# Both mixers' output products as seven half-size products, in a two-layer fp32 decoder kernel on one NeuronCore

## The chip, the core and the metric

One core of one Trainium2 chip runs the whole kernel. The metric is device time in microseconds (us) of one execution. A profiled execution is a further run, and its trace gives the start and end of every instruction on the engines PE (matrix products), PEld (its weight loads), DVE (vector), ACT (scalar, activations), POOL (GpSimd) and SP (which issues most transfers).

## What is computed

A decoder trunk of two layers on 512 positions of width 1024, in fp32. Each layer has three sub-layers, each wrapped as `x = x + RMSNorm_post(f(RMSNorm_pre(x)))`: a mixer, attention into 256 memory rows, and a SwiGLU feed-forward. The change touches the mixers' last product, `[..] @ w_out`, and the stage behind it, the keys and values of the memory.

```
def fox_shortconv_mixer(h, w_in, b_f, conv_w, w_out):      # layer 0
    ...
    y_b = b_gate * causal_depthwise_conv(c_gate * u, conv_w)
    return jnp.concatenate([y_a, y_b], axis=-1) @ w_out
def rglru_mixer(h, w_in, conv_w, conv_b, w_a, b_a, w_i, b_i, lam, w_out):   # layer 1
    gate, u = jnp.split(h @ w_in, 2, axis=-1)
    ...
    y = jax.nn.gelu(gate) * hs.astype(h.dtype)
    return y @ w_out
def memory_cross_attention(h, m, w_q, w_kv, w_o):
    q = (h @ w_q).reshape(bsz, seq, MEM_HEADS, MEM_HEAD_DIM)
    k, v = jnp.split(m @ w_kv, 2, axis=-1)
    ...
```

## The kernel before

**Products.** Every fp32 operand is split into a rounded high half and the rest, `lo = v - hi` (`split_out`, L539: ACT rounds, DVE subtracts), and a product is three matmuls, hi·hi, hi·lo and lo·hi. Weights come through four `st` buffers (SP's queue) and are split into pools `wh` and `wl` of four buffers each; a load of 128 x 1024 values is one `st`. PSUM is used as two sets of four banks, `bankA` and `bankB`.

**Order.** PE's instructions run in the order of the code. DVE, ACT and POOL are put in order by a scheduler at build time, except in a few stretches that are written out by hand (layer 1's mixer is one). SP issues loads in order, each as soon as its `st` buffer is free.

**Layer 0's mixer** (`fox`). Products of the input weights, the short convolution (`conv`) and the attention's 128-query blocks are woven: `main` yields products, `side` attention steps. The output product (`OutProj`, from L552) makes columns 0 to 511 first (`half0_steps`, 96 matmuls of 128x512: 8 k-blocks, 4 row tiles, 3 matmuls), as each quarter of `y` comes ready, then columns 512 to 1023 (`half1`, 96 more), with the post-norm of each row tile (`chain`), the next sub-layer's pre-norm (`next`) and its transposes (`transpose`) after each tile. The four loads of the second half are kept (`rh`, `rl`).

**Memory.** In layer 0 `memory_T` transposes the normalised memory rows on PE (`turn`, eight transposes each, L1001), writes them to DRAM for layer 1, and multiplies by `g_mem`. The two turns are called from `half1` behind its first two row tiles, and use `bankA`. `memory_kv` makes four chunks of 256 key columns (48 matmuls of 128x256 each), then the two remaining row tiles' transposes (`rest`), then the values (two halves of 48 matmuls of 128x512).

**Layer 1's mixer** (`rglru`). Column chunks of `c_w_in` are multiplied one after the other (`ws_gemm`), with the gates' products and the scan between; `gelu(n, ...)` makes 256 columns of `y`. After the last, `ws_gemm(w, 768, ..)`, the output product runs as in layer 0 with the bank sets exchanged.

**The feed-forward's down product** (`DownProj`, a subclass) is made in the form that the change brings to the mixers: seven products instead of eight, with weight sums `t1` to `t4` in DRAM. `plan` queues the sums' making: copies go to SP's queue between loads (`pace`: three for every four loads), adding transfers to POOL's queue (`spend`).

Of the kernel before, what the change touches and what calls it, by code (L numbers as in the profile page):

```python
# [42 lines left out]
def trunk_kernel(ctx: ExitStack, tc: tile.TileContext, a: dict, out: bass.AP):  # L43
# [103 lines left out]
    def spend(n, behind=None):  # L147
# [15 lines left out]
        ("gm", a["g_mem"].rearrange("l (m p) -> (l m) p", p=P)),  # L163
        ("gp", a["g_mix_pre"][1].rearrange("(m p) -> m p", p=P)),
    )
    off = {}
# [151 lines left out]

    def put_T_pair(hT, hss, j, gain):

        ps = bankB()
        for kk in range(2):
            for t in range(2):
                c = 2 * kk + t
                src = hss[t][j // 2][:, (j % 2 * 2 + kk) * P:(j % 2 * 2 + kk + 1) * P]
                nc.tensor.transpose(out=ps[:, c * P:(c + 1) * P], in_=src, identity=ident)
        ks = [(2 * j + kk, ps[:, kk * 256:kk * 256 + 256]) for kk in range(2)]
        for k, v in ks:
            nc.scalar.mul(out=hT.hi[k][:, 0:256], in_=v, mul=ch(gain, k))
        for k, v in ks:  # L330
            nc.vector.scalar_tensor_tensor(out=hT.lo[k][:, 0:256], in0=v, scalar=ch(gain, k), in1=f(hT.hi[k][:, 0:256]),
                                           op0=ALU.mult, op1=ALU.subtract)

# [324 lines left out]
    class DownProj(OutProj):  # L658
# [300 lines left out]
        def hook(self, m):  # L959
# [3 lines left out]
            elif m == 3:  # L963
                self.transpose(3)


    memT = dram.tile([P, KT, MEM], F32, name="memT")
# [54 lines left out]

    def memory_kv(layer, vhi, vlo, between):

# [14 lines left out]
        between()  # L1039
        vh, vl = group("vh"), group("vl")  # L1040
        for nh in range(2):
# [10 lines left out]
            for j in range(2):  # L1052
                split_out(banks[j], vh[:, 2 * j + nh, :], vl[:, 2 * j + nh, :])
        return kh, kl, vh, vl

# [148 lines left out]
    def fox(proj):  # L1204
# [124 lines left out]

        y = Feat([None] * KT, [None] * KT)  # L1330
        yg, qk, cs = {}, {}, {}
        done = set()
        TO = [(0, 0), (1, 0), (2, 0), (1, 384)]

        def y_group(m):
            if m not in yg:
                yg[m] = group("y")
                y.hi[m], y.lo[m] = yg[m][:, 0, :], yg[m][:, 1, :]
                y.hi[4 + m], y.lo[4 + m] = yg[m][:, 2, :], yg[m][:, 3, :]
            return yg[m]  # L1340

        def qk_pairs(m0):


            def put_q(banks):
                for i in range(2):
                    qk[m0 + i] = group("qk")
                    split_out(banks[i], qk[m0 + i][:, 0, :], qk[m0 + i][:, 1, :], -0.125)

            def put_k(banks):  # L1350
                for i in range(2):
                    split_out(banks[i], qk[m0 + i][:, 2, :], qk[m0 + i][:, 3, :])
                    done.add(("qk", m0 + i))

            yield from ws_steps(w, m0 * P, hT, put_q)
            yield from ws_steps(w, FOXW + m0 * P, hT, put_k)

        def attention(m):
# [53 lines left out]

            yt, tmp = sbuf("yt"), sbuf("tmp")
            for s in range(2):
# [11 lines left out]
                yield 1  # L1426
            gy = y_group(m)
            split_out(yt, gy[:, 0, :], gy[:, 1, :])
            done.add(("y", m))

        def conv(m0):
# [3 lines left out]
            def put_c(banks):  # L1435
                for i in range(2):
                    cs[m0 + i] = sbuf("cs")
                    nc.scalar.copy(out=cs[m0 + i], in_=banks[i])

            def put_u(banks):  # L1440
                for i in range(2):
                    c = cs[m0 + i]
                    t = sbuf("cu", 514)
                    nc.gpsimd.memset(t[:, 0:2], 0.0)
                    nc.vector.tensor_tensor(out=t[:, 2:514], in0=banks[i], in1=c, op=ALU.mult)
                    cw = [ch("scw", 4 * j + m0 + i) for j in range(3)]
                    nc.vector.tensor_scalar_mul(out=c, in0=t[:, 2:514], scalar1=cw[2])
# [7 lines left out]
            def put_b(banks):  # L1455
                for i in range(2):
                    c = cs[m0 + i]
                    nc.vector.tensor_tensor(out=c, in0=c, in1=banks[i], op=ALU.mult)
                    gy = y_group(m0 + i)
                    split_out(c, gy[:, 2, :], gy[:, 3, :])  # L1460

# [21 lines left out]
        for _ in qk_pairs(0):  # L1483
            pass
        proj.y = y
        weave(main(), side())


    def rglru(hT, prev, proj):
        w = a["c_w_in"][0]  # L1490
        U, PU, Q = {}, {}, {}
        y = Feat([None] * KT, [None] * KT)

# [16 lines left out]
        def gates(n):  # L1510
# [6 lines left out]
            for i in range(2):  # L1517
                for m in range(2):
# [5 lines left out]
                    banks[i, m] = ps  # L1524
            Qf, Pf = f(Q[n]), f(PU[n])
            for m in range(2):
                c = 2 * n + m
# [16 lines left out]
        def gelu(n, banks):  # L1544
            yg = group("y")
            Qf = f(Q[n])
            for m in range(2):
# [6 lines left out]
                nc.vector.scalar_tensor_tensor(out=s, in0=s, scalar=1.0, in1=gp, op0=ALU.add, op1=ALU.mult)  # L1554
                nc.vector.tensor_tensor(out=s, in0=s, in1=Qf[:, m, :], op=ALU.mult)
                split_out(s, yg[:, m, :], yg[:, 2 + m, :], 0.5)
                y.hi[2 * n + m], y.lo[2 * n + m] = yg[:, m, :], yg[:, 2 + m, :]

# [12 lines left out]
        gelu(2, ws_gemm(w, 512, hT))  # L1571
        gelu(3, ws_gemm(w, 768, hT))
        proj.y = y
        proj.half0(range(0, KT, 2), True, True)


    hT = prev = None
    for layer in range(2):
        hTc = new_hT() if layer else None
        pf = DownProj(layer, a["g_ffn_post"][layer], a["g_mix_pre"][1], None, layer == 1)  # L1580
        pf.follow_w = a["c_w_in"][0], (D, D + 256)
        pf.plan()
        pm = OutProj(a["ab_w_out"][0] if layer == 0 else a["c_w_out"][0], None, KT,
                     a["g_mix_post"][layer], a["g_cross_pre"][layer], hTc, *((bankA, bankB) if layer == 0 else (bankB, bankA)))
        if layer == 0:
            fox(pm)
            pm.hT = hTc = new_hT()
        else:
            rglru(hT, prev, pm)
        vhi, vlo, steps = memory_T(layer, pm.first)  # L1590
        pm.half1(steps)
        pm.next(NT - 1)
        spend(1)

        def rest():
            for t in (2, 3):
                pm.transpose(t)

        kv = memory_kv(layer, vhi, vlo, rest)
        hTf = new_quads()  # L1600
# [30 lines left out]
```

## Time and profile before

| | us |
|---|---|
| median of 3 runs | 1390.49 (1390.46 to 1390.69) |
| the profiled execution | 1390.6 |
| its span, first to last instruction | 1388.8 |
| mean granted PE clock, share of full | 0.996 |
| attention's last product to the memory's first transposes, layer 0 | 195.02 to 214.15 |
| layer 0's key products | about 234 to 257 |
| layer 1's output product, first to last matmul with `wh` | 842.0 to 863.1 |

Lines of the profile name an engine, a line, an operation and `out<-in`. Behind a group stand its count, busy time and mean nanoseconds, then the idle time of the engine ahead of it and what ended that. Matmuls overlap, so a matmul's own duration (0.39 us for 128x512) is longer than the distance between two starts, which is what one more costs.

### The profile page before, as it was taken

The page shows a single profiled execution, that of the slowest core. Times are in us where ns is not written, and L with a number is a line of the kernel's source. Part 1 is how long each engine was busy: PE and PEld are TensorE (multiplying, and loading weights), DVE is VectorE, ACT ScalarE, POOL GpSimd, SP SyncE. Part 2 cuts the span into 40 slices and gives each one's busy share as a digit, 9 for nine tenths or more (in the row PEclk, how much of TensorE's full clock was granted, in tenths as well). Part 3 has the DMA queues.
Part 4 walks back from the last instruction along what each step waited for, and adds up shares of the span by engine and source line. Part 5 has one row for each costly group of instructions (what it writes and reads, how often), then busy time and mean ns, then how long its engine had stood idle before and what let it go on. Part 6 is the DMA issues. An engine that isn't in the chain of part 4 may idle for free.

```text
span 1388.8 us, 21766 instructions
## 1 busy us (share of the span) xinstructions
PE 1375.6 (99%) x8416; PEld 1225.7 (88%) x8416; DVE 1110.5 (80%) x1801; ACT 725.3 (52%) x1187; POOL 111.7 (8%) x161
## 2 busy tenths in 40 slices
PE   8999999999999999999999999999999999999997
PEld 6778788988899999998889888988889999999886
DVE  6876677646589999989898999663568999999987
ACT  4354456434465444456674797453456444445663
POOL 1000002011010101000011000101200011000001
PEclk9999999999999999999999999999999999999999
DMA  6844452667424567566665657256812555666653
GB/s 225 277 156 158 139 178 66 210 158 148 106 92 137 155 158 186 159 231 229 196 220 178 223 169 248 82 185 153 166 61 92 168 152 174 153 176 239 208 188 132
DMA packets 155250, 233.62 MB, mean 168 GB/s; under 512 B 8477, under 2 KB 90497, under 8 KB 153866
## 3 DMA queue, kind: packets, MB, share of 16 engines
q1 hardware_dynamic: 134706, 180.25, 40.1%
q0 software_dynamic: 17072, 46.16, 15.2%
q10 hardware_dynamic: 3368, 5.82, 1.3%
q8 instruction: 66, 1.08, 0.3%
q14 instruction: 38, 0.31, 0.1%
HBM read 219.60 MB, written 58.74 MB: 200 GB/s over the span
## 4 chain that ended last, share of the span: by engine, by line
PE 98%; DMA 1%; issue 1%; DVE 0%; POOL 0%; SPq 0%; ACT 0%; DVEq 0%; POOLq 0%
PE bA L336 14%; PE bA L338 14%; PE bA L337 14%; PE bB L336 6%; PE bB L337 6%; PE bB L338 6%; PE bB L810 3%; PE bB L812 3%; PE bB L811 3%; PE bA L810 2%; PE bA L812 2%; PE bA L811 2%; PE bA L569 2%; PE bA L571 2%; PE bB L571 2%; PE bB L569 2%
## 5 line engine op out<-in xcount | busy, mean ns | idle before, releaser
L546 DVE TENSOR_TENSOR wl<-st,wh 128x1024 fp32r<-128x1024 f32 x108 | 131.2, 1221 | 96.2 <-ACT wh L545 94.9
L545 ACT CAST wh<-st 128x1024 fp32r<-128x1024 f32 x108 | 113.1, 1050 | 119.5 <-PE bA L337 70.2
L336 PE MATMUL bA<-hTh,wh 128*128 128x512 f32 (+1 forms) x448 | 171.4, 383 | 0.2 <-ACT hTh L314 0.2
L337 PE MATMUL bA<-hTl,wh 128*128 128x512 f32 (+1 forms) x448 | 167.8, 375 | 0.3 <-DVE hTl L315 0.3
L338 PE MATMUL bA<-hTh,wl 128*128 128x512 f32 (+1 forms) x448 | 168.1, 375 | 0.0
L437 ACT CAST wg<-wr 128x1024 fp32r<-128x1024 f32 x80 | 83.6, 1045 | 49.1 <-DVE wr L466 38.4
L776 ACT CAST wh<-st 128x1024 fp32r<-128x1024 f32 x76 | 74.9, 985 | 63.6 <-PE bA L812 27.0
L338 PEld LDWEIGHTS bA<-hTh,wl 128*128 128x128 f32 x448 | 84.3, 188 | 15.4
L438 DVE TENSOR_TENSOR wg<-wr,wg 128x1024 fp32r<-128x1024 f32 x80 | 97.1, 1214 | 0.0
L337 PEld LDWEIGHTS bA<-hTl,wh 128*128 128x128 f32 x448 | 84.6, 189 | 14.1 <-DVE hTl L315 0.5
L336 PEld LDWEIGHTS bA<-hTh,wh 128*128 128x128 f32 x448 | 84.5, 189 | 14.0 <-ACT hTh L314 0.5
L781 DVE TENSOR_TENSOR wl<-st,wh 128x1024 fp32r<-128x1024 f32 x76 | 86.1, 1133 | 10.2 <-ACT wh L776 10.2
L437 ACT CAST wh<-tt 128x1024 fp32r<-128x1024 f32 x40 | 42.1, 1053 | 61.4 <-DVE tt L466 61.4
L336 PE MATMUL bA<-hTq,wh 128*128 128x256 f32 x208 | 59.2, 284 | 0.0
L338 PE MATMUL bA<-hTq,wl 128*128 128x256 f32 x208 | 58.8, 283 | 0.0
L337 PE MATMUL bA<-hTq,wh 128*128 128x256 f32 x208 | 58.8, 283 | 0.0
L810 PE MATMUL bB<-wh,ya 128*128 128x512 f32 x148 | 57.6, 389 | 0.0
L811 PE MATMUL bB<-wl,ya 128*128 128x512 f32 x148 | 57.6, 389 | 0.0
L812 PE MATMUL bB<-wh,ya 128*128 128x512 f32 x148 | 57.6, 389 | 0.0
L756 DVE TENSOR_TENSOR ya<-yb,ya 128x512 fp32r<-128x512 f32 x84 | 53.3, 638 | 0.0
L810 PE MATMUL bA<-wh,ya 128*128 128x512 f32 x132 | 51.3, 389 | 0.0
L811 PE MATMUL bA<-wl,ya 128*128 128x512 f32 x132 | 51.3, 389 | 0.0
(375 smaller groups left out, 4428.4 us busy)
## 6 DMA issues: line engine op xcount, KB each, us to landing
wr<-in_w_ffn_gu_dram SPq DMA_DIRECT2D x80, 512.0 KB
st<-t SPq DMA_DIRECT2D x40, 512.0 KB
t<-in_w_ffn_down_dram SPq DMA_DIRECT2D x32, 512.0 KB
st<-in_w_xkv_dram SPq DMA_DIRECT2D x32, 512.0 KB
st<-in_w_ffn_down_dram SPq DMA_DIRECT2D x30, 512.0 KB
st<-in_ab_w_in_dram SPq DMA_DIRECT2D x24, 512.0 KB
y<-yr POOLq DMA_DIRECT2D x18, 512.0 KB, 3.9
t<-in_w_ffn_down_dram POOLq DMA_DIRECT2D x16, 512.0 KB, 8.7
```

The lines of the kernel that those rows point to most:

```text
L336: nc.tensor.matmul(out=ps, lhsT=wh, rhs=xh, start=first, stop=False)
L337: nc.tensor.matmul(out=ps, lhsT=wh, rhs=xl, start=False, stop=False)
L338: nc.tensor.matmul(out=ps, lhsT=wl, rhs=xh, start=False, stop=last)
L437: return (lambda: nc.scalar.copy(out=to[0], in_=src), lambda: nc.vector.tensor_tensor(out=to[1], in0=src, in1=f(to[0]), op=ALU.subtract))
L438: lambda: nc.vector.tensor_tensor(out=to[1], in0=src, in1=f(to[0]), op=ALU.subtract))
L545: nc.scalar.copy(out=hi, in_=src)
L546: nc.vector.tensor_tensor(out=lo, in0=src, in1=f(hi), op=ALU.subtract)
L776: nc.scalar.copy(out=self.wt[s][0], in_=self.st[s])
L781: nc.vector.tensor_tensor(out=lo, in0=self.st[s], in1=f(hi), op=ALU.subtract)
L810: nc.tensor.matmul(out=banks[t], lhsT=yh, rhs=wh[:, jj, :], start=first and jj == 0, stop=False)
L811: nc.tensor.matmul(out=banks[t], lhsT=yh, rhs=wl[:, jj, :], start=False, stop=False)
L812: nc.tensor.matmul(out=banks[t], lhsT=yl, rhs=wh[:, jj, :], start=False, stop=last and jj == n - 1)
```

## The change

Both output products become a `MixProj`. With the mixer's output cut into row halves 1, 2 and inner halves 1, 2 (`a11` to `a22`) and the weights likewise (`b11` to `b22`), seven products of 256 rows, 512 inner and 512 columns are formed (24 matmuls of 128x512 each, 168 in all where there were 192) from `n3 = a21 - a11`, `s2 = a22 - n3`, `n1 = a11 - s2`, `n4 = a12 - s2` and the weight sums. They are made in fourteen pieces of twelve matmuls:

| pieces | 0, 1 | 2, 3 | 4, 6 | 5, 7 | 8, 9 | 10, 11 | 12, 13 |
|---|---|---|---|---|---|---|---|
| product | a11·b11 | n3·t3 | a22·t4 | a12·b21 | s2·t2 | n1·t1 | n4·b22 |

Each piece loads and splits one 128 x 1024 block of weights: fourteen splits where there were eight. The sums take eight copies and eight adds per mixer. Activations: DVE makes the differences and splits each of the seven operands; after the products it combines them (`q`, `v`, `c21`, `p1`). The norm steps behind that (`tail`) are called between the key chunks of `memory_kv` (c = 0 to 3) and after the first half of the values; the gain of the next pre-norm is applied at the transposes, by channel, so that its own load is gone.

In layer 0 pieces take the place of `half0_steps`; a11, n3, a22, a12 lie in `bankA`, s2, n1, n4 in `bankB`, and the memory's turns go on using `bankA`. In layer 1 pieces 0 and 1 go ahead of `ws_gemm(w, 768, ..)`, and the sets are exchanged. The first key chunk's weights are loaded ahead (`ahead`).

```diff
+    class MixProj(DownProj):
+        PIECES = tuple((n, j) for n in ("a11", "n3") for j in range(2)) + tuple(
+            (n, j) for j in range(2) for n in ("a22", "a12")) + tuple((n, j) for n in ("s2", "n1", "n4") for j in range(2))
+        B = {"a11": "b11", "n3": "t3", "a22": "t4", "a12": "b21", "s2": "t2", "n1": "t1", "n4": "b22"}
...
+        SUMS = {"n3": ("a21", "a11"), "s2": ("a22", "n3"), "n1": ("a11", "s2"), "n4": ("a12", "s2")}
...
+        def plan(self):
+            for to, frm, add in (("t3", "b12", "b22"), ("t2", "b11", "t3"), ("t4", "b21", "t2"), ("t1", "b11", "b12")):
+                for js in ((0, 2), (2, 4)):
+                    copies.append(lambda to=to, frm=frm, js=js: nc.sync.dma_start(
+                        out=self.rows(to, *js), in_=self.rows(frm, *js)))
+                    adds.append(lambda to=to, add=add, js=js: nc.gpsimd.dma_start(
+                        out=self.rows(to, *js), in_=self.rows(add, *js), accum_op=ALU.add))
...
+        def piece(self, s):
+            name, j = self.PIECES[s]
+            self.need(s + 2)
+            if j == 0:
+                self.bk[name] = [self.bank_of[name]() for _ in range(2)]
...
+        def finish(self, turns, ahead):
+            tt = lambda o, i0, i1, op: nc.vector.tensor_tensor(out=o, in0=i0, in1=i1, op=op)
+            bk, two = self.bk, range(2)
+            self.run(8, 9)
+            for o in ("n1", "n4"):
+                self.sub(o)
+                self.split(o)
+            turns[0]()
+            self.need(12)
+            for t in two:
+                tt(self.q[t], bk["s2"][t], self.p1[t], ALU.subtract)
+            self.run(10, 11)
+            for t in two:
+                tt(self.v[t], self.v[t], self.q[t], ALU.add)
+                tt(self.c21[t], bk["a22"][t], self.v[t], ALU.subtract)
+                self.square(t, 0, self.c21[t])
+            for t in two:
+                tt(self.p1[t], bk["a12"][t], self.p1[t], ALU.add)
+                self.square(2 + t, 0, self.p1[t])
+            turns[1]()
+            ws = ahead()
...
+            self.run(12, 13)
+            return ws
+        def tail(self, c):
+            two = range(2)
+            if c == 0:
...
+                for t in two:
+                    self.gain(0, self.c21[t])
+                    self.gain(1, self.v[t])
+                    self.root(t)
+                    self.add(t, (self.c21[t], self.v[t]))
+            elif c == 1:
...
+                self.pairs(0)
```

In `memory_kv`, inside the loop over the chunks `c`:

```diff
-            ws = w_chunk(w, c * 256)
...
+            if c < 3:
+                ws = w_chunk(w, (c + 1) * 256)
+            between(c)
```

In `fox`, in `main`:

```diff
-            yield from proj.half0_steps((4, 6), True, False)
+            yield from proj.piece(0)
+            yield from proj.piece(1)
+            proj.keep("a11")
+            yield from proj.piece(2)
+            yield from proj.piece(3)
+            proj.keep("n3")
             yield lambda: ("y", 1) in done
-            yield from proj.half0_steps((0,), False, False)
+            for m in range(2):
+                proj.split2(m)
+            yield from proj.piece(4)
+            yield from proj.piece(5)
             yield lambda: ("y", 3) in done
-            yield from proj.half0_steps((2,), False, True)
+            for m in range(2, 4):
+                proj.split2(m)
+            proj.sub("s2")
+            proj.split("s2")
+            yield from proj.piece(6)
+            yield from proj.piece(7)
```

In `rglru`, at its end, and where the layers are called:

```diff
-        gelu(3, ws_gemm(w, 768, hT))
-        proj.y = y
-        proj.half0(range(0, KT, 2), True, True)
+        proj.run(0, 1)
+        b3 = ws_gemm(w, 768, hT)
+        proj.keep("a11")
+        proj.need(3)
+        gelu(3, b3)
+        proj.run(2, 3)
+        proj.keep("n3")
+        proj.run(4, 5)
+        proj.sub("s2")
+        proj.split("s2")
+        proj.run(6, 7)
...
+    BANKS = [{n: bankB if n in late else bankA for n in MixProj.B} for late in (("s2", "n1", "n4"), ("a11", "n3", "a22", "a12"))]
...
-        pm.half1(steps)
...
+        ws = pm.finish(steps, lambda: w_chunk(a["w_xkv"][layer], 0))
...
+        kv = memory_kv(layer, vhi, vlo, ws, pm.tail)
```

The built order shows where the scheduler put the steps. The first place is DVE in layer 0 between the attention's last add (L1425 before, L1602 now) and the operations behind the memory's rows (`mem`); `y`, `yl`, `yp` are the low halves of the mixer's output, `c_a` and `c_n` the combined results. Before:

```order
L1425 TENSOR_TENSOR yt<-bB,tmp 64x512
L546 TENSOR_TENSOR y<-yt,y 128x512
L546 TENSOR_TENSOR wl<-st,wh 128x1024 x2
L592 TENSOR_TENSOR ya<-bA,gain 128x512
L224 TENSOR_SCALAR post<-post 128x1
L592 TENSOR_TENSOR ya<-bA,gain 128x512 x3
L224 TENSOR_SCALAR post<-post 128x1 x3
L546 TENSOR_TENSOR wl<-st,wh 128x1024
L224 TENSOR_SCALAR mem<-mem 128x1
L228 SCALAR_TENSOR_TENSOR mem<-mem 128x1
L982 TENSOR_SCALAR mem<-mem 128x512 x2
L224 TENSOR_SCALAR mem<-mem 128x1
```

Now:

```order
L547 TENSOR_TENSOR wl<-st,wh 128x1024
L1160 TENSOR_SCALAR mem<-mem 128x512 x2
L225 TENSOR_SCALAR mem<-mem 128x1
L1012 TENSOR_TENSOR yr<-yr 128x4x256
L229 SCALAR_TENSOR_TENSOR mem<-mem 128x1
L547 TENSOR_TENSOR wl<-st,wh 128x1024
L1160 TENSOR_SCALAR mem<-mem 128x512 x2
L547 TENSOR_TENSOR yp<-yr,yp 128x4x256
L1080 TENSOR_TENSOR c_a_1839<-bB,c_a_1839 128x512 x2
L547 TENSOR_TENSOR wl<-st,wh 128x1024
L1080 TENSOR_TENSOR c_n_1909<-c_n_1909,c_a_1839 128x512 x2
L1080 TENSOR_TENSOR c_n_1909<-bA,c_n_1909 128x512 x2
```

Where the memory's rows stood among post-norm work (`ya`, `post`), they stand now among operand splits (`yp`), differences (`yr`) and the combining. The first subtraction in the last row (`c21`, L1080) frees the bank that PE's transposes of `mem` are to be written to; these have the same place on PE as before, behind 84 matmuls.

The second place is SP's queue in layer 1 around the last chunk of `c_w_in` (768 on) and the first loads of `c_w_out`; `t_1` is a buffer of the feed-forward's sums, `mt_1` the sums of the mixer. Before:

```order
L119 DMA st<-in_c_w_in_dram 128x4x256
L694 DMA t_1_7442<-in_w_ffn_down_dram 128x2x512
L119 DMA st<-in_c_w_in_dram 128x4x256
L694 DMA t_1_7441<-in_w_ffn_down_dram 128x2x512
L119 DMA st<-in_c_w_in_dram 128x4x256 x2
L694 DMA t_1_7443<-in_w_ffn_down_dram 128x2x512
L119 DMA st<-in_c_w_out_dram 128x2x512
L694 DMA t_1_7440<-in_w_ffn_down_dram 128x2x512
L119 DMA st<-in_c_w_out_dram 128x2x512
```

Now:

```order
L1040 DMA st<-in_c_w_out_dram 128x2x512
L695 DMA t_1_7537<-in_w_ffn_down_dram 128x2x512
L1040 DMA st<-in_c_w_out_dram 128x2x512
L695 DMA t_1_7539<-in_w_ffn_down_dram 128x2x512
L1040 DMA st<-mt_1_126 128x2x512 x2
L695 DMA t_1_7536<-in_w_ffn_down_dram 128x2x512
L119 DMA st<-in_c_w_in_dram 128x4x256
L695 DMA t_1_7538<-in_w_ffn_down_dram 128x3x512
L119 DMA st<-in_c_w_in_dram 128x4x256
L695 DMA t_1_7537<-in_w_ffn_down_dram 128x3x512
```

The chunk's two loads have moved behind the first four loads of the output product.

The third is DVE in layer 1 at the first key chunks, where each low half of keys (`kl`) follows its chunk's splits. Before:

```order
L546 TENSOR_TENSOR wl<-st,wh 128x1024 x2
L546 TENSOR_TENSOR kl<-bA,kh 128x512
L546 TENSOR_TENSOR wl<-st,wh 128x1024 x2
L546 TENSOR_TENSOR kl<-bA,kh 128x512
L546 TENSOR_TENSOR wl<-st,wh 128x1024 x2
L546 TENSOR_TENSOR kl<-bA,kh 128x512
L546 TENSOR_TENSOR wl<-st,wh 128x1024 x2
L546 TENSOR_TENSOR kl<-bA,kh 128x512
```

Now:

```order
L547 TENSOR_TENSOR kl<-bA,kh 128x512
L831 SCALAR_TENSOR_TENSOR x_110<-c_n_8651,post,x_110 128x512 x2
L225 TENSOR_SCALAR post<-post 128x1
L547 TENSOR_TENSOR wl<-st,wh 128x1024
L229 SCALAR_TENSOR_TENSOR post<-post 128x1
L547 TENSOR_TENSOR wl<-st,wh 128x1024
L831 SCALAR_TENSOR_TENSOR x_111<-c_n_8651,post,x_111 128x512 x2
L547 TENSOR_TENSOR kl<-bA,kh 128x512
L225 TENSOR_SCALAR pre<-pre 128x1 x2
L822 TENSOR_TENSOR c_a_8587<-c_a_8587,gain 128x512
L229 SCALAR_TENSOR_TENSOR pre<-pre 128x1 x2
L822 TENSOR_TENSOR c_a_8587<-c_a_8587,gain 128x512 x3
```

Adds into x, statistics and gains stand now between the weight splits of the key chunks, where only splits stood.

More of the change, by code (lines that the diff above doesn't have):

```diff
@@ L1021, in memory_T, with memory_kv @@
         return vhi, vlo, (lambda: turn(0), last)
-    def memory_kv(layer, vhi, vlo, between):
+    def memory_kv(layer, vhi, vlo, ws, between):
         w = a["w_xkv"][layer]
@@ L1445, in put_u @@
                     nc.vector.tensor_tensor(out=t[:, 2:514], in0=banks[i], in1=c, op=ALU.mult)
+                    if m0 and i:
+                        spend(3, t[:, 2:3])
                     cw = [ch("scw", 4 * j + m0 + i) for j in range(3)]
@@ L1456, in put_b @@
                 for i in range(2):
[L1457 to L1460, printed above, removed]
+                    nc.vector.tensor_tensor(out=proj.act(0, m0 + i), in0=cs[m0 + i], in1=banks[i], op=ALU.mult)
+                proj.first_pair(m0 // 2)
             yield from ws_steps(w, base + FOXW, hT, put_c)
```

162 lines of the change are left out of this document (130 added, 32 removed).

## The prediction

> **What bounds the kernel now.** The page's busy times, its chain and PE's waits come first.
>
> ```profile
> PE 1375.6 (99%) x8416; PEld 1225.7 (88%) x8416; DVE 1110.5 (80%) x1801; ACT 725.3 (52%) x1187; POOL 111.7 (8%) x161
> PE 98%; DMA 1%; issue 1%; DVE 0%; POOL 0%; SPq 0%; ACT 0%; DVEq 0%; POOLq 0%
> PE bA L1231 <- ACT hTh L314: 1.5, 1, 1.5
> PE bB L1218 <- POOL ident masks.py:199: 1.5, 1, 1.5
> PE bB L305 <- DVE h L258: 1.2, 2, 0.6
> PE bA L337 <- DVE hTl L315: 0.3, 1, 0.3
> PE bA L336 <- ACT hTh L314: 0.2, 1, 0.2
> ```
>
> PE is busy 99 % of the span, the chain is PE, and its waits in the whole program come to 1.5 + 1.5 + 1.2 + 0.3 + 0.2 = 4.7 us. Each matmul taken away is worth its pitch, as long as PE goes on finding its operands. The second engine is DVE at 80 %, so I looked at the stretches that the change touches (start and end, length, then busy time of PE, PEld, DVE, ACT, POOL, then the clock, DMA share and GB/s).
>
> ```profile
> 195.02:214.15 19.13, 19.13 (x86) 15.78 (x86) 10.48 (x20) 9.79 (x21) 0.56 (x1) 1.00 0.50 158
> 800.00:846.00 46.00, 46.00 (x205) 38.09 (x204) 44.65 (x64) 39.39 (x53) 0.00 (x0) 1.00 0.59 193
> 880.00:915.00 35.00, 35.00 (x259) 33.29 (x258) 24.03 (x37) 17.91 (x32) 3.93 (x6) 1.00 0.46 136
> ```
>
> At the end of layer 0's attention DVE has 10.48 of 19.13 us of work; in layer 1's gates and gelus 44.65 of 46.00, level with PE; in layer 1's key products 24.03 of 35. The change adds DVE work in all three.
>
> **The gain.** 48 matmuls of 128x512 go, 24 in each mixer (192 to 168). Their starts:
>
> ```profile
> 201.00 0.39 PE L571 MATMUL bA<-wh,y 128*128 128x512 f32 x1
> 206.44 0.39 PE L571 MATMUL bA<-wh,y 128*128 128x512 f32 x1
> 234.21 0.28 PE L336 MATMUL bA<-mTh,wh 128*128 128x256 f32 x1
> 256.88 0.28 PE L336 MATMUL bA<-mTh,wh 128*128 128x256 f32 x1
> 214.15 1.03 PE L1001 MATMUL bA<-ident,mem 128*128 128x128 f32 x8
> 257.24 1.47 PE L305 MATMUL bB<-ident,h 128*128 128x128 f32 x12
> ```
>
> 24 of them start between 201.00 and 206.44: 0.2267 us each, so **−10.9 us**. For what follows: 189 key products of 128x256 take 22.67 us, 0.12 each; eight transposes last 1.03 and twelve 1.47, 0.11 each.
>
> **What DVE costs.** One row for each kind of instruction (count, then busy us and mean ns), and two neighbours in time:
>
> ```profile
> L546 DVE TENSOR_TENSOR wl<-st,wh 128x1024 fp32r<-128x1024 f32 x108 | 131.2, 1221 | 96.2 <-ACT wh L545 94.9 <-PE bB L1405 0.6
> L423 DVE TENSOR_TENSOR raw<-raw 128x1024 f32<-128x1024 f32 x8 | 9.7, 1219 | 3.3 <-ACT raw L311 3.3
> L850 DVE TENSOR_TENSOR c<-bB,c 128x512 f32<-128x512 f32 x16 | 10.8, 682 | 4.7 <-PE bB L812 4.7
> L830 DVE SCALAR_TENSOR_TENSOR x<-c,post,x 128x512 f32<-128x512 f32 x12 | 8.6, 743 | 0.7 <-POOL post L232 0.7
> L1010 DVE SCALAR_TENSOR_TENSOR mTl<-mTr,chan,mTh 128x256 fp32r<-128x256 f32 x16 | 6.5, 475 | 0.0
> L331 DVE SCALAR_TENSOR_TENSOR hTl<-bB,chan,hTh 128x256 fp32r<-128x256 f32 x8 | 3.3, 474 | 0.5 <-ACT hTh L329 0.5
> L982 DVE TENSOR_SCALAR mem<-mem 128x512 f32<-128x512 f32 x4 | 1.8, 483 | 1.5 <-POOL mem L232 1.5
> L1542 DVE TENSOR_TENSOR_SCAN q<-pu,q 128x512 f32<-128x512 f32 x8 | 9.3, 1207 | 0.0
> L1551 DVE TENSOR_SCALAR ge<-ge 128x512 f32<-128x512 f32 x8 | 3.3, 418 | 0.0
> L228 DVE SCALAR_TENSOR_TENSOR post<-post 128x1 f32<-128x1 f32 x24 | 3.7, 155 | 4.0 <-ACT junk L220 3.4
> 839.32 0.68 DVE L1555 TENSOR_TENSOR ge<-ge,q 128x512 f32<-128x512 f32 x1
> 839.92 0.68 DVE L1552 TENSOR_TENSOR ge<-ge,bA 128x512 f32<-128x512 f32 x1
> ```
>
> So: 1.22 for 1024 columns (weight split, subtraction or split of an operand), 0.68 for 512, 0.74 for an add into x, 0.475 for 256 columns with a gain, 0.48 for a scaled memory row, 1.21 a scan, 0.42 a scalar operation, 0.16 a column of statistics. Neighbours of 0.68 start 0.60 apart, so I take 0.08 off per instruction. A weight split waits 94.9/108 = 0.88 for ACT's rounding on average; that is my price of one wait.
>
> **Stall A, layer 0, the memory's transposes.** The order has 84 matmuls between the last attention product and the eight transposes of `mem`, as before; they take the 19.13 us of the first window (84 × 0.2267 = 19.0). The transposes now take banks that a22 held, and these come free at `c21`, 31 DVE instructions after the last attention add.
>
> ```profile
> 194.73 0.45 PE L1421 MATMUL bB<-pT,v 128*128 128x256 f32 x3
> 196.22 0.69 DVE L1425 TENSOR_TENSOR yt<-bB,tmp 64x512 f32<-64x512 f32 x1
> ```
>
> That add starts 1.2 us after PE goes on to the next product at 195.02. The 31: thirteen of 1.22 (seven weight splits, three subtractions, three operand splits), ten of 0.68, four memory rows of 0.48, four of 0.16: 25.2, less 31 × 0.08: 22.7. PE gets there at 19.1, DVE at 1.2 + 22.7 = 23.9: **floor 4.8**. With four of the seven weight splits waiting for ACT (3.6) I take **8.4**; all seven give 11.0. Behind the transposes on PE stand n1, n4 and all key products.
>
> **Stall B, layer 0, key products.** From there to the first value product DVE has eleven weight splits, twenty of 0.68, eight adds into x, sixteen of 0.475 and sixteen of 0.16: 43.1, less 71 × 0.08: 37.4. PE has 48 matmuls (10.9), 192 key products (23.0), 32 transposes (3.5): 37.4. Level, so floor 0; one wait, **0.9**, is taken, three (2.6) is the end.
>
> **Stall C, layer 1, the last gelu's columns.** Pieces 0 and 1 stand ahead of the product of columns 768 on, and SP loads their weights, and those of 2 and 3, ahead of its chunks. All four `st` buffers are held until DVE has split piece 0, and the chunk's low half comes fifteen DVE rows later: from piece 0's split on, five of 1.22, nine of 0.68, two scans, two of 0.42: 15.5, less 18 × 0.08: 14.0. Less piece 0's own split (1.1) and PE's pieces 0 and 1 (24 × 0.2267 = 5.4) leaves **7.5**. Behind that product on PE stand the other 144 of the mixer; on SP the loads of t3's pieces stand behind the chunk's, held by the same four buffers. The row of 800 to 846 says that DVE is level with PE there, so it has no lead to spend. With two more half-size subtractions and a split ahead of piece 0 (2 × 0.68 + 1.22) it could be 10.1.
>
> **Stall D, layer 1, key products.** From `q` to the first value split: ten weight splits, 26 of 0.68, eight adds into x, twelve of 0.475, fifteen of 0.16: 44.0, less 71 × 0.08: 38.3, starting 0.4 late. PE: 48 matmuls (10.9), 192 key products (23.0), sixteen transposes (1.8): 35.7. **Floor 3.0**; with two or so waits of 0.88 I take **5.0**, with five 7.4. The value products, the query and the attention stand behind.
>
> **The clock.** The rows of the start show what an idle PE costs:
>
> ```profile
> 6.87:10.28 3.41, 1.48 (x9) 0.84 (x8) 1.26 (x3) 1.37 (x2) 0.00 (x0) 1.00 1.02 402
> 10.28:13.69 3.41, 3.20 (x8) 2.44 (x9) 3.13 (x8) 2.78 (x6) 0.00 (x1) 0.50 1.05 404
> ```
>
> After 3.41 us with PE busy only 1.48, the granted clock is 0.50 for the next 3.41: 1.7 us lost. Stalls A, C and D are long enough, 0 to 5.1 us; as DVE goes on meanwhile and is the one behind, I take **1.5**. The Trainium skill, page "TensorE: Matmul & The Clock Gate", section "Part 1: The HAM clock gate", says that the clock halves after an idle window of about 3.4 us and comes back after a busy one; the half clock's length agrees, the window ahead of it was not wholly idle. If by that rule only a window with no work at all counts, the stalls here, each made of shorter waits, cost no clock and the sum would be +10.9.
>
> **What is hidden.** The weight sums (eight copies on SP's queue, eight adds on POOL's for each mixer) touch no engine that is waited for. Their room:
>
> ```profile
> L1445 DVE TENSOR_TENSOR cu<-bA,cs x4: 673/682/684, 89.7 to 169.8; 128x512 f32<-128x512 f32 x4
> t<-in_w_ffn_down_dram POOLq DMA_DIRECT2D x16, 512.0 KB, 8.7
> ```
>
> The last of t4's adds is issued behind the last `cu` at 169.8 and should land some 9 us later (8.7 is the row of a like transfer); its piece comes after the last attention products, at 195. POOL, 8 % busy, issues the adds ahead of the next `cu` fills and attention biases; SP's copies stand among loads that it issues ahead of need (DMA share 0.50 to 0.59 in these windows). ACT's new copies and gains (52 % busy) lie beside PE. If that cover goes, it is a rival below.
>
> **Sum.** −10.9 + 8.4 + 0.9 + 7.5 + 5.0 + 1.5 = **+12.4**. Against the profiled execution's 1390.6 us (the span of 1388.8 and 1.8 around it; the median of the runs, 1390.49, is the same within 0.1) that is **1403.0**.
>
> **Rivals.**
> 1. *Only the floors* (15 %): DVE never waits for ACT and the clock stays. 4.8 + 0 + 7.5 + 3.0 = 15.3, +4.4, **1395.0**. For it: ACT is half idle. Against it: the wait of 0.88 at each weight split is what the row of before has.
> 2. *DVE keeps up* (7 % faster, 5 % within 0.2 %): the whole saving, **1379.7**. It would take DVE through its 75 us of stretches A, C and D (22.7 + 14.0 + 38.3) in 60. It decides from stalls below 8.1 us in all, about 10 % off that time. For it: DVE is idle 20 % of the span and could enter a stretch ahead. Against: 44.65 of 46.00 before C, the split of 1221 ns that 108 instances give, and in A it cannot start ahead of the attention's last add.
> 3. *The sums come late* (7 %): POOL's adds are slowed while DVE is busy. t4 then lands after 169.8 + 25, and PE waits before its second piece. It decides from three times the 8.7 us; at five times (43.5) t4 comes at 213, 18 us late: **1421**. Against it: that 8.7 was itself measured in a program whose DVE is 80 % busy. The Trainium skill, page "SBUF — State Buffer", section "Who interferes with whom", describes just that: transfers issued by GpSimd held up by certain DVE operations, about 620 to 3100 ns. The 8.7 us here neither shows nor excludes it.
>
> **How the numbers follow.** The forecast has 66 %. All upper ends (11.0, 2.6, 10.1, 7.4 and 5.1, less 10.9) give +25.3, 1415.9, all of them together being unlikely. The range 1393 to 1413 takes in the forecast and the floors, and leaves out rivals 2 and 3 and the far end. A measurement of this kernel tells about 0.2 % (2.8 us) from no change. Faster 7 %, same 5 %, slower 66 + 15 + 7 = 88 %.
>
> **What would show it.** In the changed profile PE's busy time falls by about 11 us and its waits grow from 4.7 to some 25. They should be: `bA<-ident,mem` waiting for a DVE subtraction near 215 us (A); layer 1's columns 768 waiting for `wh`/`wl` just after the first 24 products of the mixer (C); first key and value products of layer 1 waiting for ACT's `wh` and DVE's `wl` (D). A PE wait on a load of the `mt` sums would mean rival 3. No wait above 2 us in these places would make me wrong, and rival 2 right.

## The result, and the profile after

| | before, us | with the change, us |
|---|---|---|
| median | 1390.59 | 1415.37 |
| lowest to highest run | 1390.46 to 1391.88 | 1413.86 to 1416.91 |
| profiled execution (span) | 1390.6 (1388.8) | 1416.91 (1414.9) |

The change makes the kernel slower: the ratio is 1.0176, 95 % interval 1.0158 to 1.0194. The forecast of 1403 had the direction and the places, and half the size: +12.4 where +24.8 was measured, outside its range. The profiled execution is the slowest of the four runs, 1.5 above their median, and its span is 26.1 longer than that of before; what is read from traces below belongs to those 26.1.

The page of the changed kernel, engines and chain:

```profile
PE 1375.3 (97%) x8368; PEld 1222.3 (86%) x8368; DVE 1147.8 (81%) x1857; ACT 758.1 (54%) x1245; POOL 142.2 (10%) x184
PE 83%; DVE 5%; issue 5%; DMA 4%; ACT 3%; POOL 0%; SPq 0%; DVEq 0%; POOLq 0%; ACTq 0%
```

48 matmuls fewer, and PE is busy as long as before: the saved 10.9 us have been spent on slower matmuls, most of them at half clock, as the windows below show. DVE has 37 us more to do (1110.5 before), and the chain leaves PE for 17 % of the span. What PE waited for (total, times, longest), without the waits at the program's start:

```profile
PE bA L1179 <- DVE c_n L1080: 9.6, 1, 9.6
PE bA L339 <- DVE wl L547: 4.7, 1, 4.7
PE bA L1229 <- DVE wl L547: 3.3, 1, 3.3
PE bA L337 <- ACT wh L546: 2.3, 1, 2.3
PE bB L1055 <- ACT wh L546: 1.8, 1, 1.8
...
PE bA L337 <- DVE c_n L1080: 1.6, 1, 1.6
...
PE bB L1056 <- DVE wl L547: 0.8, 1, 0.8
```

Each is where the prediction put a stall. The first is A, the memory's transposes (L1179) waiting for `c21`. L339 and L337 behind `wl` and `wh`, with L1055 and L1056 (piece 0) ahead of them, are C: 9.6 in all. L1229 and L337 behind `c_n` are D, 4.9. B (L327, 0.2) is absent.

The windows of stall A, 3.41 us each and counted on from those of the program's start (their edges lie some 0.1 us ahead of the changes of the clock, hence 0.52 and 0.98), and the first window behind it, show the other part (busy time of PE, PEld, DVE, ACT, POOL; clock, DMA share, GB/s):

```profile
218.49:221.91 3.42, 0.00 (x0) 0.00 (x0) 2.98 (x6) 1.99 (x2) 1.40 (x1) 1.00 1.07 391
221.91:225.32 3.41, 0.00 (x0) 0.00 (x0) 3.38 (x6) 0.00 (x0) 0.00 (x0) 0.52 1.06 397
225.32:228.73 3.41, 2.20 (x10) 2.11 (x11) 3.41 (x6) 2.13 (x6) 0.00 (x0) 0.50 0.94 322
228.73:232.15 3.42, 3.42 (x10) 2.65 (x9) 2.27 (x8) 1.50 (x5) 0.00 (x0) 0.50 0.29 110
232.15:235.56 3.41, 3.41 (x16) 2.81 (x15) 1.37 (x2) 1.05 (x1) 0.00 (x0) 0.98 0.00 0
```

While PE stands still DVE is busy nearly without a gap. The clock goes to half behind the empty window and comes back only when a window has been busy from end to end (2.20 of 3.41 was not enough): ten matmuls start in 228.73 to 232.15, sixteen in the next. PE goes on at 226.5 (2.20 ahead of 228.73), so it works 5.6 us at half clock and loses 2.8. The same in layer 1, at C (853.37 on) and D (931.87 on):

```profile
853.37:856.78 3.41, 0.00 (x0) 0.00 (x0) 3.08 (x6) 2.81 (x5) 0.00 (x0) 0.52 0.69 244
856.78:860.20 3.42, 2.15 (x5) 1.79 (x6) 3.42 (x5) 0.86 (x2) 0.00 (x0) 0.50 1.00 329
860.20:863.61 3.41, 3.41 (x9) 2.67 (x9) 0.13 (x1) 0.00 (x0) 0.00 (x0) 0.50 1.04 388
...
931.87:935.29 3.42, 0.61 (x3) 0.52 (x4) 3.28 (x9) 2.55 (x7) 1.71 (x2) 1.00 0.00 0
935.29:938.70 3.41, 3.41 (x10) 2.65 (x9) 2.81 (x3) 2.34 (x4) 2.08 (x2) 0.52 0.78 238
```

C's products resume at 858.04 (quoted below), so 5.6 us at half clock, 2.8 lost; D's single window loses 1.7. With A that is 7.3 us.

In C the chain of the changed kernel (time, length, what) goes through a transfer:

```profile
846.83 7.04 DMA st<-in_c_w_in_dram
...
853.97 1.04 ACT wh L546
855.01 0.53 ACT yh L546
...
855.57 0.57 DVE yl L547
...
856.17 0.68 DVE ge L1743
856.86 1.15 DVE wl L547
...
858.04 0.80 PE bA L339
```

The chunk's second load is issued when piece 1's split has given its buffer back, and takes 7.04 us. Meanwhile DVE works through the rows of its order, reaching the chunk's low half at 856.86. DVE's row sets the end: from 843.50 to that split DVE stands idle once, for 0.33 us behind ACT's `yh`, so a faster load could have brought no more than that in this order.

### The profile page after: what moved, and what is told of

It is laid out like the page before. It is cut to its first block, busy times and chain, and to the rows that moved or that the text cites. A ratio compares the mean times of both kernels' runs of the same rounds, so it can differ in the third digit from the quotient of the medians.

```text
span 1414.9 us, 21903 instructions
## 1 busy us (share of the span) xinstructions
PE 1375.3 (97%) x8368; PEld 1222.3 (86%) x8368; DVE 1147.8 (81%) x1857; ACT 758.1 (54%) x1245; POOL 142.2 (10%) x184
## 4 chain that ended last, share of the span: by engine, by line
PE 83%; DVE 5%; issue 5%; DMA 4%; ACT 3%; POOL 0%; SPq 0%; DVEq 0%; POOLq 0%; ACTq 0%
PE bA L339 11%; PE bA L337 11%; PE bA L338 11%; PE bB L337 5%; PE bB L338 5%; PE bB L339 5%; PE bB L813 3%; PE bB L811 3%; PE bB L812 3%; PE bA L813 2%; PE bA L811 2%; PE bA L812 2%; DMA st<-in_c_w_in_dram 2%; DVE wl L547 1%; PE bA L1229 1%
## 5 line engine op out<-in xcount | busy, mean ns | idle before, releaser
L547 DVE TENSOR_TENSOR wl<-st,wh 128x1024 fp32r<-128x1024 f32 x128 | 155.0, 1222 | 93.4 <-ACT wh L546 92.7
L546 ACT CAST wh<-st 128x1024 fp32r<-128x1024 f32 x128 | 133.9, 1052 | 121.0 <-PE bA L338 62.8
L337 PE MATMUL bA<-hTh,wh 128*128 128x512 f32 (+1 forms) x448 | 172.5, 385 | 2.5 <-ACT wh L546 2.3
L339 PE MATMUL bA<-hTh,wl 128*128 128x512 f32 (+1 forms) x448 | 169.4, 378 | 4.7 <-DVE wl L547 4.7
L777 ACT CAST wh<-st 128x1024 fp32r<-128x1024 f32 x76 | 74.9, 986 | 63.7 <-PE bA L813 27.0
L339 PEld LDWEIGHTS bA<-hTh,wl 128*128 128x128 f32 x448 | 85.0, 190 | 20.8 <-DVE wl L547 5.2
L337 PEld LDWEIGHTS bA<-hTh,wh 128*128 128x128 f32 x448 | 85.2, 190 | 16.7 <-ACT wh L546 2.7
L782 DVE TENSOR_TENSOR wl<-st,wh 128x1024 fp32r<-128x1024 f32 x76 | 86.7, 1141 | 10.1 <-ACT wh L777 10.1
L233 POOL TENSOR_TENSOR post<-post,nhalf 128x1 f32<-128x1 f32 x24 | 17.3, 721 | 435.1 <-DVE post L229 435.1
L337 PE MATMUL bA<-hTq,wh 128*128 128x256 f32 x208 | 59.2, 284 | 0.0
L339 PE MATMUL bA<-hTq,wl 128*128 128x256 f32 x208 | 58.8, 283 | 0.0
```

What stands on the lines that cost most here:

```text
L337: nc.tensor.matmul(out=ps, lhsT=wh, rhs=xh, start=first, stop=False)
L339: nc.tensor.matmul(out=ps, lhsT=wl, rhs=xh, start=False, stop=last)
L546: nc.scalar.copy(out=hi, in_=src)
L547: nc.vector.tensor_tensor(out=lo, in0=src, in1=f(hi), op=ALU.subtract)
L777: nc.scalar.copy(out=self.wt[s][0], in_=self.st[s])
L782: nc.vector.tensor_tensor(out=lo, in0=self.st[s], in1=f(hi), op=ALU.subtract)
```

## The experiments

Each line has the median of its runs and the kernel before on the same chip.

| | edit | us | before, us | ratio, 95 % interval |
|---|---|---|---|---|
| e1 | memory's transposes early, layer 0 | 1423.49 | 1390.92 | 1.0228 (1.0213 to 1.0243) |
| e2 | last chunk ahead of pieces 0, 1, layer 1 | 1405.93 | 1390.92 | 1.0108 (1.0093 to 1.0123) |
| e3 | norm steps shifted | 1414.42 | 1390.92 | 1.0162 (1.0147 to 1.0177) |
| e4 | weight sums left out | 1409.78 | 1390.92 | 1.0137 (1.0120 to 1.0154) |
| e5 | e1, with the memory's loads ahead | 1411.45 | 1390.90 | 1.0152 (1.0137 to 1.0168) |
| e6 | norm steps shifted, second way | 1408.77 | 1390.90 | 1.0135 (1.0120 to 1.0150) |
| e7 | e2 + e6 + transposes behind n1 | 1398.84 | 1390.90 | 1.0052 (1.0035 to 1.0069) |
| e8 | e2 + e6 + e5 | 1391.99 | 1390.90 | 1.0006 (0.9997 to 1.0016) |
| e9 | e8 + two edits in layer 1 | 1394.53 | 1390.69 | 1.0029 (1.0020 to 1.0038) |
| e10 | the change, stall A filled with idle matmuls | 1412.13 | 1390.69 | 1.0154 (1.0140 to 1.0167) |
| e11 | layer 0 alone, with e5 and e6 | 1388.17 | 1391.05 | 0.9980 (0.9971 to 0.9989) |
| e12 | layer 0 alone | 1397.90 | 1391.05 | 1.0051 (1.0036 to 1.0067) |

**The layers apart (e12).** Layer 1's mixer and the steps behind it are those of the kernel before:

```diff
+        pm = OutProj(a["c_w_out"][0], None, KT, a["g_mix_post"][1], a["g_cross_pre"][1], hTc, bankB, bankA) if layer else mixers[0]
```

> The change in layer 0 alone, as it was made, with layer 1's mixer and the steps behind it as in the kernel before. Theory (two separate places of loss, some 13 us in layer 0 and 22 in layer 1, less 5.4 saved in each): 1390.7 - 5.4 + 13 = 1398, 1396 to 1400. Rival (the two layers' losses hang together, by the sums' transfers or the clock): outside 1394 to 1402.

Measured 1397.9, as the theory has it. Layer 0 costs +6.9, that is 12.3 us lost for 5.4 saved; the rest of +24.8, some 18, goes with layer 1 and its sums, which this run leaves out as well. The split is rough: in this run stall A is 8.2 us instead of 9.6, and the half clock behind it is shorter (3.3 us, PE going on at 224.21):

```profile
224.12:227.54 3.42, 3.33 (x12) 3.04 (x13) 3.42 (x9) 3.26 (x9) 0.00 (x0) 0.50 0.48 164
227.54:230.95 3.41, 3.41 (x16) 2.81 (x16) 1.35 (x5) 1.43 (x3) 0.00 (x0) 1.00 0.00 0
```

**Is DVE what PE waits for (e10).** 38 matmuls without use stand where PE is idle in stall A:

```diff
+            if not self.layer:
+                self.bk["n1"] = [self.bank_of["n1"]() for _ in range(2)]
+                for _ in range(38):
+                    nc.tensor.matmul(out=self.bk["n1"][0], lhsT=self.parts["s2"][0][:, 0, 0:P],
+                                     rhs=self.second[0][:, 0, :], start=True, stop=True)
             turns[0]()
```

> The change with 38 further matmuls of 128x512 (8.6 us) on PE between s2's products and the memory's transposes in layer 0, into the bank that n1's product then overwrites: they fill the wait of 9.6 us with work that nobody needs. Theory (DVE sets the end there, and the wait also costs clock): no us is added, and the half clock of the products behind (1.9 us) does not come, 1 to 3 us less than the change, 1412 to 1415, with the granted clock at 1.00 behind the transposes. Rival (PE's own work or a transfer sets the end there): 5 to 9 us more, 1420 and above.

8.6 us of further work made the program 3.2 us faster than the change. The windows of that stretch:

```profile
217.40:225.70 8.30, 7.85 (x35) 6.18 (x33) 7.82 (x12) 2.00 (x2) 1.40 (x1) 1.00 1.06 376
225.70:232.00 6.30, 6.13 (x31) 5.07 (x32) 5.57 (x13) 4.92 (x11) 0.00 (x0) 1.00 0.55 185
```

DVE is as busy as in the change, PE no longer stands still, and the clock stays at 1.00. So DVE sets the end of the stall, and the half clock is a price of its own: 3.2 measured, 2.8 read from the windows, and 2.9 by the traces from the first product behind the attention to the query product (90.9 us here, 93.8 in the change).

**The bank (e1, e5).** The transposes move ahead of piece 0; in e5, shown here, the memory's rows are loaded a product stage earlier too (in e1 the call of `memory_T` stands behind `conv(2)`):

```diff
+            proj.mem = memory_T(0, bankA)
             yield from conv(2)
+            for turn in proj.mem[2]:
+                turn()
+                yield 2
             yield from proj.piece(0)
```

> Layer 0's memory rows are transposed ahead of piece 0, while free banks are there, so the sixteen transposes no longer wait for the subtraction that frees a22's banks. Theory (the wait of 9.6 us is a bank held until DVE has come through its row): the wait and the half clock behind it (1.9 us lost) vanish, about 1 us comes back where n4 waits for s2's banks: 9 to 11 us less than the change, 1404 to 1407. Rival (DVE is late as a whole and PE waits for the next thing just as long): less than 4 us gained, a new wait on n1, n4 or the first key chunk.

> As the first experiment, but the memory rows' loads and norm are called one product stage earlier, ahead of the second half of the short convolution. Theory (the first experiment's new wait of 8.5 us was the rows' load, queued on SP behind a weight load that had to wait for its buffer, and not DVE's amount of work): that wait falls below 2 us and the bank wait stays away: 8 to 11 us less than the change, 1404 to 1408. Rival (DVE's amount of work in layer 0 is what counts): the lost time comes back at another product of layer 0, less than 4 us gained.

e1 is 8 us slower than the change. The bank's wait is gone, and in its place stands, in e1's waits and chain:

```profile
PE bA L1181 <- DVE mem L1162: 8.5, 1, 8.5
...
180.82 6.73 DMA mem<-in_mem_dram
187.58 0.72 ACT junk L221 x2
```

SP issued the memory's rows only at 180.82, behind the load of t4's second half; PE asked for them at 183. The expectation of e5 says that this load had to wait for its buffer. The trace names the weight sum instead: POOL issued t4's last add at 171.32, and SP's queue stood until it had landed:

```profile
171.32 1.21 POOL L997 DMA_DIRECT2D mt<-mt  x1
...
SPq L1040 <- DMA mt<-mt: 7.9, 1, 7.9
...
180.42 0.36 SPq L1040 DMA_DIRECT2D st<-mt  x1
```

In e5 PE's wait is gone (12 us faster than e1), and still only 3.9 of the 8 to 11 expected are gained on the change. e5's waits say where the rest went:

```profile
PE bA L1231 <- DVE wl L547: 6.8, 2, 3.5
...
PE bB L327 <- ACT h L847: 2.4, 2, 2.2
```

The value product's wait for its weights now stands in both layers (3.5 at most, 6.8 together, where it was 3.3 in layer 1 alone). In the change stall A may have given DVE those microseconds; that wasn't tried. So the rival's number and place held: taking one wait away brought up the next. Its cause, the amount of DVE's work, did not: e11, below, has that work with the steps in another order, and neither wait is left.

**The last chunk (e2).**

```diff
-        proj.run(0, 1)
         b3 = ws_gemm(w, 768, hT)
+        proj.run(0, 1)
         proj.keep("a11")
```

> In layer 1 the product of columns 768 on goes back ahead of pieces 0 and 1. Theory (the order of the loads and of DVE's row made the stall): the two waits in that product (2.5 and 4.9 us), its half clock (2.7 us) and most of the 3.0 us ahead of and in piece 0 go: 9 to 12 us less than the change, 1403 to 1407. Rival (DVE is simply level with PE there and the split of the sums' weights comes late in any order): the wait moves to pieces 0 to 3, less than 4 us gained.

9.4 us less than the change: the wait of 4.7 is 0.5, those of piece 0 are gone, one of 1.8 is left ahead of the chunk. The order made stall C. (About one of the 9.4 is stall A, 8.5 in this run, which the edit doesn't touch.)

**The key products (e3, e6).** In e3 the gains and adds of row tiles 2 and 3 go behind the fourth chunk, and the second half's transposes behind the values:

```diff
             elif c == 3:
+                for t in two:
+                    self.gain(0, self.p1[t])
+                    self.gain(1, self.q[t])
+                    self.root(t + 2)
+                    self.add(t + 2, (self.p1[t], self.q[t]))
```

> The gains and adds of row tiles 2 and 3 move from between the second and third key chunk to behind the fourth, and the second half's transposes behind the whole value product. Theory (DVE's row ahead of the first value weights is too long by some 3 us): four gains and four adds, 5.1 us net, leave that row; the 3.5 us wait of the first value product and the half clock (1.7) behind it go: 4 to 6 us less, 1409 to 1412. Rival (the work has to be done before the query product anyway): the wait moves to the query, within 2 us of the change.

No gain that can be told: the value wait fell to 1.0, and the transposes wait for their rows:

```profile
PE bB L327 <- ACT h L847: 2.3, 2, 1.4
...
PE bA L1228 <- DVE pre L225: 1.0, 1, 1.0
```

e6 also moves the transposes of both halves into the two value products and splits the first value weights ahead of the last steps:

```diff
+            else:
+                first = load_w(w, 0, 2, D, 512)
             between(c)
...
+                if k2 == 4:
+                    between(4 + nh)
```

> The first value weights are split ahead of the last norm steps, the transposes of both halves move into the two value products, gains of tiles 2 and 3 behind the third key chunk and their adds behind the fourth. Theory (the value product waits because its weights' split stands behind norm steps; experiment 3 failed by the transposes, which came before their rows were ready): value wait and half clock of layer 1 (3.5 and 1.7) and the waits on `h` vanish: 4 to 6 us less, 1409 to 1412. Rival: the query waits for the second half's transposes instead, within 2 us of the change.

6.6 us less than the change, a little more than expected, with a value wait of 0.8. Stall D was the order of the steps, as the theory has it. Of the 6.6, 1.7 are stall A, 7.9 in this run, which stands ahead of the edit.

**All together (e7, e8, e9).** In e7 the transposes of layer 0 go behind n1's pieces, in e8 ahead of piece 0 as in e5; both have the edits of e2 and e6.

> Three edits together: the chunk ahead of pieces 0 and 1, the shifted steps, and in layer 0 both groups of memory transposes behind n1's pieces. Theory: the second experiment's 9.4 us, some 5 of the shifted steps, and of the 9.6 us wait the 5.4 that n1's 24 products cover, with the half clock behind it: 19 to 24 us less than the change, 1392 to 1396. Rival (the waits give way to others): above 1400.

> Three edits together: chunk first, shifted steps, and the memory's transposes early with their loads ahead. Theory: 9.4 + 5 + 9 to 11 less than the change, 1389 to 1393, level with the kernel before; the rest of the saving of 10.9 us is held by the waits ahead of the last chunk in layer 1 (3 us) and small ones. Rival (work that DVE must do anyway): above 1397.

e7 ends 16.5 us below the change, 2.8 above its range; of the bank's wait 2.5 us are left. e8 ends 23.4 below the change, level with the kernel before: the mended order pays back 23 us, and the 10.9 of the saving are still spent, on small waits, most of them in layer 1, and on one more window of half clock there, behind the wait of 2.4 (the last two lines below):

```profile
PE bA L337 <- DVE c_n L1080: 2.4, 1, 2.4
PE bA L337 <- ACT wh L546: 1.8, 1, 1.8
...
PE bB L337 <- ACT q L1727: 0.9, 1, 0.9
...
882.54:885.95 3.41, 1.46 (x12) 1.49 (x13) 3.41 (x6) 1.71 (x4) 0.00 (x0) 1.00 0.73 233
885.95:889.36 3.41, 3.41 (x18) 3.41 (x18) 3.41 (x5) 1.13 (x4) 0.00 (x0) 0.50 0.67 220
```

e9 takes two of these away: n3's difference and split behind the last chunk, and the first key chunk of layer 1 in a bank that is free sooner.

```diff
-            self.split("n3", js)
...
         b3 = ws_gemm(w, 768, hT)
+        proj.sub("n3")
+        proj.split("n3")
...
+            ps = bankB() if layer and c == 0 else bankA()
```

> Experiment 8 with two more edits in layer 1: n3's difference and split behind the last chunk's product instead of beside the first two gelus (2.7 us of DVE less while DVE is level with PE), and the first key chunk in a bank that a22 held, which is free before n1's. Theory: the waits of that product (2.5 us in all) mostly go, and the 2.4 us of the first key chunk for n1's bank goes: 3 to 5 us less than experiment 8, 1387 to 1389, faster than the kernel before. Rival (DVE has too much to do from there on): the waits come back at pieces 2 and 3 or the second key chunk, within 1.5 us of 1392.

2.5 us slower than e8, which is outside both ranges; the rival, with its 1.5 us either way, is the nearer. The wait for n1's bank is gone, and PE waits for weights: in the last chunk's product, which the theory had relieved (2.3), at a key chunk (1.4) and at the values.

```profile
PE bA L339 <- DVE wl L547: 3.7, 2, 2.3
...
PE bA L1235 <- ACT wh L546: 1.6, 1, 1.6
PE bA L1236 <- DVE wl L547: 1.5, 2, 0.8
```

**Layer 0 alone, mended (e11).**

> The seven products in layer 0 alone, with the early transposes and the shifted steps of experiments 5 and 6; layer 1's mixer and the steps behind it as in the kernel before. Theory (in layer 0 DVE has the room once nothing waits for a bank; in layer 1 it has not): 24 matmuls less (5.4 us) and some 3 us of small waits left, as experiment 8 shows for layer 0: 1387.5 to 1389.5, faster than the kernel before by 1 to 3 us. Rival: the new order costs layer 0 as much as it saves, 1390 to 1393.

1388.17, faster than the kernel before by 0.2 % with an interval that leaves 1 out. Its page reads:

```profile
PE 1371.4 (99%) x8392; PEld 1221.0 (88%) x8392; DVE 1128.0 (81%) x1829; ACT 740.6 (53%) x1216; POOL 127.6 (9%) x173
```

PE is at 99 % again with 24 matmuls less. From 195 to 262 us PE is busy 66.49 of 67.00 and DVE 59.91, so in layer 0 DVE has the room. This version beats both kernels.

**The sums (e4).** `t1` to `t4` are replaced by `b11`, `b11`, `b12` and `b21`, and neither copied nor added:

```diff
-            return self.sums[name].rearrange("(j p) n -> p j n", p=P)[:, j0:j1, :]
+            return self.rows({"t1": "b11", "t2": "b11", "t3": "b12", "t4": "b21"}[name], j0, j1)
```

> The weight sums of both mixers are left out, copies and adds, and the pieces read unsummed weights in their place, so both mixers' outputs are other numbers. Theory (DVE's rows and the order make the stalls, the transfers lie beside them): within 3 us of the change, 1412 to 1418. Rival (the extra transfers make the loads late, the 7 us in which the chain follows a load of c_w_in): 8 us or more less, below 1408.

5.6 us less than the change: between the two. Piece 0's wait of 1.8 for ACT's `wh` is gone, which every run with the change's order and the sums has; C's 4.4 and D's 3.3 stay. A's wait is 8.2 instead of 9.6, but e2 and e6, which keep the sums, have 8.5 and 7.9. The transfers are not hidden wholly, and they are not what makes the large waits; how the rest of the 5.6 divides isn't shown.

## Why the prediction was wrong

**The gain** stands as a count: 48 matmuls fewer, and e11 and e12 count 24 for one layer. Their 0.2267 us each is read from before; no run measures it by itself.

**The places of A, C and D** stand, and so does their cause for the most part: A ends when DVE has come through its row (e10), C by the order of loads and rows (e2), D by the steps ahead of the value weights (e6).

**The term that failed is the clock.** The step took 1.5 us, from a window of half clock at 1.7 and the thought that DVE, going on meanwhile, would hide most of it. Measured are 2.8 + 2.8 + 1.7 = 7.3, more than the 5.1 of the term's own upper end. The half clock falls on the products behind the wait, where PE is the bound again, and it lasts until one of the fixed windows has been busy nearly from its start to its end: 5.6 us behind A and C, not 3.4. The two rows used for it, at the program's start, showed the drop and one slow window; there PE happened to be busy 3.20 of 3.41 in it. The other reading that the prediction weighed, that only wholly idle windows count, is refuted at D: 0.61 of 3.42 busy, and then 0.52. In e8 a window with 1.46 was followed by half clock too. The rule that an idle window halves the clock and a busy one restores it (the Trainium skill, page "TensorE: Matmul & The Clock Gate", section "Part 1: The HAM clock gate") agrees with the rows of A, where a window is empty; at D and in e8 the measurement goes beyond it, since a window busy in part did the same.

**C was 9.6, not 7.5.** The chunk's own waits, 2.3 + 4.7 = 7.0, are near the step's figure. It left out the piece's own waits ahead of it, 1.8 and 0.8, which it had put into the upper end alone. The 1.8 is gone in e4, so it goes with the sums.

**A was 9.6, not 8.4.** From the attention's last add to the first subtraction for `c21` these rows of DVE and ACT stand out:

```profile
197.96 0.69 DVE L1602 TENSOR_TENSOR yr<-bB,tmp 64x512 f32<-64x512 f32 x1
...
212.88 0.63 ACT L221 ACTIVATE junk<-mem 128x512 bf16<-128x512 f32 x1 [2.69 <-DMA mem<-in_mem_dram]
213.63 0.15 DVE L225 TENSOR_SCALAR mem<-mem 128x1 f32<-128x1 f32 x1 [1.93 <-ACT junk L221]
...
225.78 1.28 DVE L1080 TENSOR_TENSOR c_n<-bA,c_n 128x512 f32<-128x512 f32 x2
```

The add's start and PE's going on at 226.53 are 28.6 us apart, where 22.7 + 3.6 = 26.3 were reckoned; PE on its side took 20.4 (196.60 to 216.97) where 19.1 were reckoned, and that hides about half of the difference. DVE's longest wait in it, 1.93, is none of the waits at weight splits that the step priced: the statistics of the memory's rows had to wait for the rows' load. The same wait is 0.55 in e4, 0.88 in e2 and 0.30 in e6, and A is 8.2, 8.5 and 7.9 there. So A's size moves with the landing of that load; since e2 and e6 keep the sums, it isn't shown that the sums delay it.

**B** was 0.2 instead of 0.9, **D** 4.9 instead of 5.0; of D, 1.6 is a wait for a bank (`c_n`) and not for weights, as the step had it. With these sizes the sum is −10.9 + 9.6 + 0.2 + 9.6 + 4.9 + 7.3 = +20.7 of the 26.1 between the two spans. The same products in both traces tell where the rest lies. The first one behind the attention starts at 195.02 before and at 196.60 now, 1.6 later; 1.3 of that is there at 43 us, where e2, e3 and e12 are within 0.2 of before, so it goes with this one execution and not with the change. The first query product starts at 280.78 and 290.36 in layer 0, 8.0 more, of which the terms give −5.4 + 9.6 + 0.2 + 2.8 = 7.2; in layer 1 at 933.95 and 959.70, another 16.2, of which they give −5.4 + 9.6 + 4.9 + 2.8 + 1.7 = 13.6. The 3.4 that are missing in the two layers hold small waits of 0.5 and 0.6 us; what else they are stays open.

**The sums were called hidden**, and the kernel without them is 5.6 us faster. Rival 3, with t4 late by 18 us, did not happen in the change: t4's second half was loaded at 182.37, ahead of the attention's end, and no wait of PE names a load of the sums. But the same add held SP's queue for 8.6 us there and for 7.9 in e1, where PE had to wait for what stood behind it.

**The range** ended at 1413, 2.4 below the median. Its upper terms gave +25.3, almost what was measured, and that is luck: the four waits stayed 6.8 below their upper ends, the clock went 2.2 above its own, and the rest of what was measured has no term. A half clock comes with a wait, so its price belongs in each wait's term and not in one of its own.

## What to carry to other kernels

Where PE is the bound, count what a product's replacement costs DVE in each stage and in its order, not in the span: 37 us more at 81 % of the span turned into waits where PE needed something that stood late in DVE's row. Price a wait together with the slow products behind it, also when it is shorter than a clock window: the 3.3 us of D and the 2.4 us in e8 were each followed by half clock. Look at what stands behind a load on its queue: in e1 a sum that came late held up rows that had nothing to do with it. A mended order paid back one stall after another, and with both layers changed the total only came level (e8); two more edits did not help (e9). Whether layer 1 has too much work for DVE or the right order wasn't found is not shown; until then keep the half of the change where the room is (e11).

## What was not expected of the hardware

The granted clock comes back after a window of 3.41 us with PE busy nearly throughout, so the price of a stall depends on where it ends in the window: 5.6 us at half clock behind A and C, 3.4 behind D, and 3.3 behind A in e12. The runs of the changed kernel spread over 3.1 us (1413.86 to 1416.91) where those of the kernel before spread over 1.4; the places of the windows may be why, which wasn't tried. 38 matmuls that nobody needs, put into an idle stretch, make the program 3.2 us faster.
